# Four sums of weight blocks in each seven-product chunk: accumulating transfers on GpSimd's queue in place of VectorE additions

## The chip, the cores and the metric

The kernel runs on one core of one Trainium2 chip. A time is the device time of one execution, in microseconds (us); with one core there is no other to wait for. The core has TensorE (PE in the profile), VectorE (DVE), ScalarE (ACT), GpSimd (POOL) and a queue that only starts transfers (SP), each of which runs its own instructions in order and waits on semaphores for the others. Sixteen DMA engines move the data of all queues.

## What is computed

A two-layer encoder over 256 positions of width 2048, all in float32. Layer 0 mixes with grouped-query attention, layer 1 with dilated sliding-window attention in three head groups; each is followed by a gated MLP of width 5632 with a width-3 convolution over positions. Cut to what matters here:

```python
D_MODEL, SEQ, DEPTH, D_FF = 2048, 256, 2, 5632

def conv_ffn(h, w_up, conv_w, conv_b, w_down):
    u = h @ w_up                                   # 256x2048 @ 2048x11264
    u = depthwise_conv3(u, conv_w) + conv_b
    gate, val = jnp.split(u, 2, axis=-1)
    return (jax.nn.silu(gate) * val) @ w_down      # 256x5632 @ 5632x2048

def reference(x, ...):
    h = x
    for i in range(DEPTH):
        hn = rms_norm(h, mix_norm[i])
        h = h + (mixer_a(hn, ...) if i % 2 == 0 else mixer_b(hn, ...))
        h = h + conv_ffn(rms_norm(h, ffn_norm[i]), w_up[i], conv_w[i], conv_b[i], w_down[i])
    return rms_norm(h, final_norm)
```

Nearly all the work is the product of 256 rows of activations with some 420 MB of weights, each weight read once.

## The kernel before

**Loads and splits.** Weights arrive in `raw` tiles of 128 partitions x 2 x 512 float32 (512 KB), loaded by SP (`load_raw`, L137; `feed`, L146). There are six such buffers (`NRAW`), handed out in turn from a list (`new_raw`, `done_raw`). TensorE works here on operands of type fp32r, so each raw tile is split (`split_raw`, L126 to L133): ScalarE copies it to a high part `wh` (L129), VectorE subtracts that from the raw tile and leaves the low part `wl` (L130). A product is then three matmuls: high by high, high by low, low by high. There are three pairs of `wh`/`wl` buffers, four in the down projections, so a split runs at most that many pieces ahead of TensorE.

**Seven-product chunks.** A chunk is 512 rows of a weight matrix (`kg`) by two column blocks of 512 (`n0`, `n1`), seen as four blocks of one raw tile each: "11" and "12" are the first half of the rows in `n0` and `n1`, "21" and "22" the second half. Instead of eight block products, a chunk does seven, with sums of blocks (a Strassen scheme). The activations' sums (`forms`) are made earlier and are not touched. In `ORDER` the products are 1, 2, 5, 3, 7, 6, 4, and on the weights' side they take

- P1: 11; P2: 21; P3: 22, as they are stored
- P5: 11 + 12 (added into the tile of 11)
- P7: 12 + 22 (added into the tile of 12)
- P6: 22 + 11 + 12 (the sum of P5 added into the tile of 22)
- P4: 21 + 22 + 11 + 12 (the sum of P6 added into the tile of 21)

A tile that is added into must have been split before, since the split reads its old contents. A product of a chunk is six matmuls of 128x512. Between the products stand ordinary column blocks ("c" units, twelve matmuls). There are 23 chunks: seven in the MLP of layer 0, eight in that of layer 1, six in the query and key projections of layer 1, two in its output projection. All other chunks of weights go through `feed` or "c" units.

**What sets the order.** `project_pair` (L216) walks through a list of units. In each pass it loads the unit's block, calls `prepare` for the next unit, splits and multiplies. `prepare` (L246) issues the addition for the next unit if that is one of P5, P7, P6, P4 (table `sums`, L239; addition in L251), at high priority, so that a scheduler puts it ahead of other VectorE work. A scheduler then orders the instructions of each engine; within an engine they run in that order. TensorE's order is that of the units.

**GpSimd** has little to do: a part of the block placing after each 32x32 transpose (`place_blocks`, L361), 49 transfers of constants and biases of at most 256 KB, and some small operations.

Of the kernel before, what the change touches and what calls it, by code (L numbers as in the profile page):

```python
# [11 lines left out]
ALU = mybir.AluOpType  # L12
AX = mybir.AxisListType

P = 128
# [12 lines left out]
AHEAD = 45  # L28
# [6 lines left out]
def tile_encoder(ctx: ExitStack, tc: tile.TileContext, x, xT, w_a, w_ao, q_gain, k_gain, w_b, w_bo,  # L35
                 rel_bias, gains, w_up, conv, w_down, final_norm, rope, ident_c, onehot, out):
    nc = tc.nc
# [29 lines left out]
    def bank(i, name):  # L67
        return psp.tile([P, 512], F32, tag=f"b{i}", name=nm(name))

    def ps_tile():  # L70
        bank_at[1] = (bank_at[1] + 1) % 4
        return bank(4 + bank_at[1], "ps")
# [18 lines left out]
    def step():  # L91
        if wide:
            for g in pending[:2]:
                if next(g, StopIteration) is StopIteration:
                    pending.remove(g)
        while pending and not wide:
            if next(pending[0], StopIteration) is not StopIteration:
                return
            pending.pop(0)
        if spare and len(pending) < 2 and next(spare[0], StopIteration) is StopIteration:  # L100
            spare.pop(0)

    def drain(keep=0):
        while len(pending) > keep:
            step()
# [10 lines left out]
    def done_raw(t):  # L116
        free_raw.append(raw_tag.pop(id(t))[0])
# [3 lines left out]
    def new_hl():  # L121
        pool, i = hl_ring.pop(0)
        hl_ring.append((pool, i))
        return [pool.tile([P, 2, 512], F32R, tag=f"{t}{i}", name=nm(t)) for t in ("wh", "wl")]

    def split_raw(r, release=True):  # L126
        wh, wl = new_hl()
        with tc.high_priority(offset=AHEAD):
            nc.scalar.activation(wh, r, AF.Copy)  # L129
            nc.vector.tensor_tensor(wl, r, wh.bitcast(F32), ALU.subtract)  # L130
        if release:
            done_raw(r)
        return wh, wl  # L133

    def load_raw(w, n, kg, s):
        r = new_raw()
        nc.sync.dma_start(r.rearrange("p a c -> p (a c)"), w[n, kg][:, s * 1024:(s + 1) * 1024])  # L137
        return r
# [38 lines left out]
    def new_acc():  # L177
        bank_at[0] = (bank_at[0] + 2) % 4
        return [bank(bank_at[0] + m, "acc") for m in range(2)]
# [36 lines left out]
    def project_pair(w, n0, n1, lhs, forms, units, late, early_done, n0_done, product_done=None, tail=False,  # L216
                     lazy=False):
        home = {1: "M1", 2: "C11", 3: "C12", 4: "C21", 5: "M5", 6: "M6", 7: "M7"}
        if product_done or lazy:
            acc = dict(zip(("C11", "C21", "C12", "C22"), new_acc() + new_acc()))  # L220
        else:
            place = ("M1", "M5", "M6", "M7", "C11", "C21", "C12", "C22")
            if tail:
                place = ("C11", "C12", "C21", "C22", "M1", "M5", "M6", "M7")
            b = bank_at[0]
            acc = {k: bank((4, 5, 6, 7, 2 - b, 3 - b, b, b + 1)[i], "acc") for i, k in enumerate(place)}

        def touched(u):
            return (home[u[2]],) if u[0] == "P" else (("C11", "C21"), ("C12", "C22"))[u[2] // 2]

        first, last = {}, {}
        for i, u in enumerate(units):
            for k in touched(u):
                first.setdefault(k, i)
                last[k] = i
        if tail:
            last["C12"] = last["C22"] = None
        blocks = {}
        sums = {5: ("11", "12"), 7: ("12", "22"), 6: ("22", "11"), 4: ("21", "22")}  # L239

        def block(kg, b):
            if (kg, b) not in blocks:
                blocks[kg, b] = load_raw(w, (n0, n1)[int(b[1]) - 1], kg, int(b[0]) - 1)
            return blocks[kg, b]

        def prepare(u):  # L246
            kind, kg, p = u
            if kind == "P" and p in sums:
                dst, src = (block(kg, b) for b in sums[p])
                with tc.high_priority(offset=AHEAD):  # L250
                    nc.vector.tensor_tensor(dst, dst, src, ALU.add)  # L251
                if p == 6:
                    done_raw(blocks.pop((kg, "11")))
                elif p == 4:
                    done_raw(blocks.pop((kg, "22")))

        last_s = max(i for i, u in enumerate(units) if u[0] == "P")
        for i, (kind, kg, p) in enumerate(units):
            if i == late:
                drain()  # L260
            if kind == "c":
                r = load_raw(w, (n0, n1)[p // 2], kg, p % 2)
            else:
                b = {1: "11", 2: "21", 3: "22", 5: "11", 7: "12", 6: "22", 4: "21"}[p]
                r = block(kg, b)
            if i + 1 < len(units):
                prepare(units[i + 1])
            wh, wl = split_raw(r, kind == "c" or p in (7, 4))
            if kind == "P" and p in (7, 4):
                blocks.pop((kg, b))  # L270
            todo = []
            if kind == "c":
                for j in range(2):
                    for m, k in enumerate(touched((kind, kg, p))):
                        todo.append((k, *at(lhs[4 * kg + 2 * (p % 2) + j], m), j))
            else:
                f = forms(kg)[p]
                for j in range(2):
                    x = f[j] if isinstance(f, list) else [t[:, j * P:(j + 1) * P] for t in f]
                    todo.append((home[p], *x, j))  # L280
            for k, *_ in todo:
                if k not in acc:
                    acc[k] = bank(4 + ("M1", "M5", "M6", "M7").index(k), "acc") if lazy else ps_tile()
            fresh = {k for k in acc if first[k] == i}
            for k, xh, xl, j in todo:
                nc.tensor.matmul(acc[k], xh, wh[:, j, :], start=k in fresh, stop=False)  # L286
                fresh.discard(k)
                nc.tensor.matmul(acc[k], xl, wh[:, j, :], start=False, stop=False)  # L288
            todo.sort(key=lambda t: (t[0], t[3]))
            for k, xh, xl, j in todo:  # L290
                nc.tensor.matmul(acc[k], xh, wl[:, j, :], start=False, stop=last[k] == i and j == 1)  # L291
            if product_done and kind == "P" and home[p][0] == "M":
                product_done(home[p], acc.pop(home[p]))
            if i == last_s:
                early_done(acc)
            if i == max(last["C11"], last["C21"]):
                n0_done(acc)
            if not (product_done or lazy) or kind == "c" or p in (1, 5, 7, 4):
                step()
        return acc  # L300
# [14 lines left out]
    def at(e, m):  # L315
        return e[m] if isinstance(e, list) else tuple(t[:, m * P:(m + 1) * P] for t in e[:2])
# [56 lines left out]
    def seven(w, n0, n1, hT, forms, units, sums, n0_ready, n1_ready):  # L373
        (k0, k1), (q0, q1) = sums

        def product_done(k, t):
            if k != "M6":
                nc.scalar.activation({"M1": k0, "M5": q1, "M7": k1}[k], t, AF.Copy)
                return
            nc.vector.tensor_tensor(q0, t, k0, ALU.add)  # L380
            nc.vector.tensor_tensor(k1, k1, q0, ALU.add)
            nc.vector.tensor_tensor(q0, q0, q1, ALU.add)
            nc.vector.tensor_tensor(q1, k1, q1, ALU.add)

        def n0_done(a):
            nc.vector.tensor_tensor(k0, a["C11"], k0, ALU.add)
            nc.vector.tensor_tensor(k1, a["C21"], k1, ALU.add)
            n0_ready([k0, k1])

        a = project_pair(w, n0, n1, hT, forms, units, None, lambda a: None, n0_done, product_done)  # L390
        nc.vector.tensor_tensor(q0, a["C12"], q0, ALU.subtract)
        nc.vector.tensor_tensor(q1, a["C22"], q1, ALU.subtract)
        n1_ready([q0, q1])
# [431 lines left out]
    def out_proj(w, slots, kgs, late, g_next, junk, pool, tags, forms=None):  # L825
# [13 lines left out]
        def pair(n0, n1, units, late_at):  # L839
            def n0_done(a):  # L840
                finished(n0, n1)
                done((a["C11"], a["C21"]), n0)

            acc = project_pair(w, n0, n1, slots, lambda kg: forms, units, late_at,
                               lambda a: start(combine(a, n0, n1, pool, "stg", combined, 2)), n0_done, lazy=True)
            done((acc["C12"], acc["C22"]), n1)
# [533 lines left out]
```

## Time and profile before

| | us |
|---|---|
| median of 2 runs | 2235.53 (2235.5 and 2235.56) |
| the profiled execution, its span | 2235.3 |
| TensorE busy | 2222.8 |
| VectorE busy | 1838.0 |
| ScalarE busy | 1549.9 |
| GpSimd busy | 329.7 |

The result lists one time for each run and none for the profiled execution beyond its span; that lies 0.2 us under the median. The granted clock is 0.999 over the span. "Busy" is the union of an engine's instructions; "idle before" is the time in which it stood still just ahead of an instruction, and the name behind it is what ended that. A row of the timeline begins with its start and its length in us, and "x8" joins eight instructions alike.

### The profile page before, as it was taken

The page shows a single profiled execution, that of the slowest core. Times are in us where ns is not written, and L with a number is a line of the kernel's source. Part 1 is how long each engine was busy: PE and PEld are TensorE (multiplying, and loading weights), DVE is VectorE, ACT ScalarE, POOL GpSimd, SP SyncE. Part 2 cuts the span into 40 slices and gives each one's busy share as a digit, 9 for nine tenths or more (in the row PEclk, how much of TensorE's full clock was granted, in tenths as well). Part 3 has the DMA queues.
Part 4 walks back from the last instruction along what each step waited for, and adds up shares of the span by engine and source line. Part 5 has one row for each costly group of instructions (what it writes and reads, how often), then busy time and mean ns, then how long its engine had stood idle before and what let it go on. Part 6 is the DMA issues. An engine that isn't in the chain of part 4 may idle for free.

```text
span 2235.3 us, 29163 instructions
## 1 busy us (share of the span) xinstructions
PE 2222.8 (99%) x10021; PEld 1840.0 (82%) x10021; DVE 1838.0 (82%) x2523; ACT 1549.9 (69%) x2393; POOL 329.7 (15%) x482
## 2 busy tenths in 40 slices
PE   9999999999999999999999999999999999999998
PEld 7888888888888888888888888888888888888886
DVE  6777778888888788979877978786887898888897
ACT  7665677777557777767876777576777754677764
POOL 2210212210001010011340213010110100001101
PEclk9999999999999999999999999999999999999999
DMA  8444656766556665666655565565566666556654
GB/s 303 164 145 151 206 189 208 243 202 191 199 197 201 200 192 176 225 204 205 212 178 191 166 206 179 188 198 187 193 195 192 197 198 211 190 193 192 227 183 151
DMA packets 126501, 437.44 MB, mean 196 GB/s; under 512 B 17313, under 2 KB 18081, under 8 KB 126353
## 3 DMA queue, kind: packets, MB, share of 16 engines
q1 hardware_dynamic: 119744, 425.64, 58.1%
q0 software_dynamic: 6176, 9.39, 1.7%
q8 instruction: 78, 1.28, 0.2%
q14 instruction: 71, 0.57, 0.1%
q10 hardware_dynamic: 432, 0.56, 0.1%
HBM read 429.20 MB, written 6.29 MB: 195 GB/s over the span
## 4 chain that ended last, share of the span: by engine, by line
PE 93%; DVE 3%; issue 1%; DMA 1%; POOL 1%; ACT 1%; SPq 0%; DVEq 0%; POOLq 0%; ACTq 0%
PE acc L155 18%; PE acc L156 18%; PE acc L154 18%; PE acc L286 11%; PE acc L291 11%; PE acc L288 11%; DVE wl L130 2%; DMA raw<-in_w_down_dram 1%; PE ps L291 1%; PE ps L321 1%; PE ps L286 1%; PE ps L288 1%; PE ps L325 0%; POOL pp L361 0%; PE ps L324 0%
## 5 line engine op out<-in xcount | busy, mean ns | idle before, releaser
L130 DVE TENSOR_TENSOR wl<-raw,wh 128x1024 fp32r<-128x1024 f32 x861 | 1056.8, 1234 | 266.4 <-ACT wh L129 262.3
L129 ACT ACTIVATE wh<-raw 128x1024 fp32r<-128x1024 f32 x861 | 902.6, 1057 | 467.5 <-PE acc L156 166.3
L154 PE MATMUL acc<-wh,xh 128*128 128x512 f32 x1664 | 649.2, 391 | 0.0
L155 PE MATMUL acc<-wl,xh 128*128 128x512 f32 x1664 | 648.8, 390 | 0.3 <-DVE wl L130 0.2
L156 PE MATMUL acc<-wh,xh 128*128 128x512 f32 x1664 | 648.1, 389 | 0.0
L155 PEld LDWEIGHTS acc<-wl,xh 128*128 128x128 f32 x1664 | 312.6, 188 | 67.4 <-DVE wl L130 2.8
L156 PEld LDWEIGHTS acc<-wh,xh 128*128 128x128 f32 x1664 | 312.4, 188 | 64.6
L154 PEld LDWEIGHTS acc<-wh,xh 128*128 128x128 f32 x1664 | 312.7, 188 | 63.7 <-ACT wh L165 0.3
L286 PE MATMUL acc<-wh,ah 128*128 128x512 f32 x762 | 297.0, 390 | 0.6 <-DVE h L544 0.6
L288 PE MATMUL acc<-wh,al 128*128 128x512 f32 x762 | 296.7, 389 | 0.0
L361 POOL COPY u<-t 32x256 f32<-32x256 f32 x176 | 110.5, 628 | 1003.9 <-DVE t L591 995.7
L291 PE MATMUL acc<-wl,ah 128*128 128x512 f32 x762 | 212.0, 389 | 0.4 <-DVE wl L130 0.4
L286 PEld LDWEIGHTS acc<-wh,ah 128*128 128x128 f32 x762 | 143.1, 188 | 31.2 <-DVE h L544 1.5
L291 PEld LDWEIGHTS acc<-wl,ah 128*128 128x128 f32 x762 | 143.0, 188 | 30.4 <-DVE wl L130 0.9
L288 PEld LDWEIGHTS acc<-wh,al 128*128 128x128 f32 x762 | 143.1, 188 | 29.5
L286 PE MATMUL acc<-wh,xh 128*128 128x512 f32 x416 | 162.7, 391 | 0.0
L288 PE MATMUL acc<-wh,xh 128*128 128x512 f32 x416 | 162.0, 389 | 0.0
L363 ACT ACTIVATE u<-t 32x256 f32<-32x256 f32 x352 | 147.6, 419 | 17.8 <-DVE t L591 9.9
L251 DVE TENSOR_TENSOR raw<-raw,raw 128x1024 f32<-128x1024 f32 x92 | 112.8, 1226 | 14.8 <-DMA raw<-in_w_down_dram 14.1
L291 PE MATMUL acc<-wl,xh 128*128 128x512 f32 x416 | 113.1, 390 | 0.0
L288 PEld LDWEIGHTS acc<-wh,xh 128*128 128x128 f32 x416 | 78.1, 188 | 16.0
L286 PEld LDWEIGHTS acc<-wh,xh 128*128 128x128 f32 x416 | 78.1, 188 | 16.0
(254 smaller groups left out, 2388.9 us busy)
## 6 DMA issues: line engine op xcount, KB each, us to landing
raw<-in_w_up_dram SPq DMA_DIRECT2D x352, 512.0 KB, 4.5
raw<-in_w_down_dram SPq DMA_DIRECT2D x176, 512.0 KB, 4.9
raw<-in_w_b_dram SPq DMA_DIRECT2D x144, 512.0 KB, 4.5
raw<-in_w_bo_dram SPq DMA_DIRECT2D x48, 512.0 KB, 4.4
raw<-in_w_a_dram SPq DMA_DIRECT2D x40, 512.0 KB, 4.5
raw<-in_w_ao_dram SPq DMA_DIRECT2D x32, 512.0 KB, 3.8
raw<-in_w_a_dram SPq DMA_DIRECT2D x16, 256.0 KB, 6.1
h<-in_x_dram SPq DMA_DIRECT2D x4, 512.0 KB, 8.4
```

The costliest lines, as they stand in the source:

```text
L129: nc.scalar.activation(wh, r, AF.Copy)
L130: nc.vector.tensor_tensor(wl, r, wh.bitcast(F32), ALU.subtract)
L154: nc.tensor.matmul(accs[m], xh, wh[:, j, :], start=st, stop=False)
L155: nc.tensor.matmul(accs[m], xh, wl[:, j, :], start=False, stop=False)
L156: nc.tensor.matmul(accs[m], xl, wh[:, j, :], start=False, stop=sp)
L251: nc.vector.tensor_tensor(dst, dst, src, ALU.add)
L286: nc.tensor.matmul(acc[k], xh, wh[:, j, :], start=k in fresh, stop=False)
L288: nc.tensor.matmul(acc[k], xl, wh[:, j, :], start=False, stop=False)
L291: nc.tensor.matmul(acc[k], xh, wl[:, j, :], start=False, stop=last[k] == i and j == 1)
L321: nc.tensor.matmul(o, lh[ls], rh[rs], start=start, stop=stop)
L361: nc.gpsimd.tensor_copy(dst, src)
L363: nc.scalar.activation(dst, src, AF.Copy)
```

## The change

`prepare` goes. In its place `sum_next` runs behind the split of a product and issues the next sum as a transfer with `accum_op=ALU.add` on GpSimd's queue: the sixteen DMA engines read the source and the destination, and write back the sum. P5's and P7's second operand is read from memory (`stored`), so blocks 12 and 22 are read twice, once to be added and once into a tile of their own; P6's and P4's is read from a tile (`flat`). Blocks 12 and 22 are also loaded earlier in the list, behind P1 and P5, and the tile of 11 is given back behind P3, that of 22 behind P6.

```diff
-        sums = {5: ("11", "12"), 7: ("12", "22"), 6: ("22", "11"), 4: ("21", "22")}
...
-        def prepare(u):
-            kind, kg, p = u
-            if kind == "P" and p in sums:
-                dst, src = (block(kg, b) for b in sums[p])
-                with tc.high_priority(offset=AHEAD):
-                    nc.vector.tensor_tensor(dst, dst, src, ALU.add)
-                if p == 6:
-                    done_raw(blocks.pop((kg, "11")))
-                elif p == 4:
-                    done_raw(blocks.pop((kg, "22")))
+        def add_onto(kg, b, src):
+            dst = blocks[kg, b].rearrange("p a c -> p (a c)")
+            nc.gpsimd.dma_start(dst, src, accum_op=ALU.add)
+
+        def stored(kg, b):
+            s = int(b[0]) - 1
+            return w[(n0, n1)[int(b[1]) - 1], kg][:, s * 1024:(s + 1) * 1024]
+
+        def flat(kg, b):
+            return blocks[kg, b].rearrange("p a c -> p (a c)")
+
+        def sum_next(kg, p):
+            if p == 1:
+                add_onto(kg, "11", stored(kg, "12"))
+                block(kg, "12")
+            elif p == 5:
+                add_onto(kg, "12", stored(kg, "22"))
+                block(kg, "22")
+            elif p == 3:
+                add_onto(kg, "22", flat(kg, "11"))
+                done_raw(blocks.pop((kg, "11")))
+            elif p == 7:
+                add_onto(kg, "21", flat(kg, "22"))
+            elif p == 6:
+                done_raw(blocks.pop((kg, "22")))
...
-            if i + 1 < len(units):
-                prepare(units[i + 1])
             wh, wl = split_raw(r, kind == "c" or p in (7, 4))
+            if kind == "P":
+                sum_next(kg, p)
```

Below, the four sums of a chunk are called sum 5, 7, 6 and 4 after the product that takes them. Lines of the changed kernel are 14 higher from here on; the transfers are issued in its L247.

First place: the second chunk (first down projection of layer 0), VectorE, before. Its tiles are 5320 (block 11), 5346 (12), 5393 (22) and 5332 (21); 5405, 5434 and 5463 are column blocks.

```order
L130 TENSOR_TENSOR wl_5396<-raw_5393,wh_5395 128x1024 [waits PE_49,Activation_49]
L307 TENSOR_TENSOR fm_5554<-xs_5551,fm_5554 128x256 [waits Activation_49]
L251 TENSOR_TENSOR raw_5393<-raw_5393,raw_5320 128x1024 [waits DVE_49]
L130 TENSOR_TENSOR wl_5409<-raw_5405,wh_5408 128x1024 [waits DMAHW3_49,PE_49,Activation_49]
L130 TENSOR_TENSOR wl_5425<-raw_5346,wh_5424 128x1024 [waits PE_49,Activation_49]
L251 TENSOR_TENSOR raw_5332<-raw_5332,raw_5393 128x1024 [waits DVE_49]
L130 TENSOR_TENSOR wl_5438<-raw_5434,wh_5437 128x1024 [waits DMAHW4_49,PE_49,Activation_49]
L130 TENSOR_TENSOR wl_5454<-raw_5393,wh_5453 128x1024 [waits PE_49,Activation_49]
L130 TENSOR_TENSOR wl_5467<-raw_5463,wh_5466 128x1024 [waits DMAHW6_49,PE_49,Activation_49]
L130 TENSOR_TENSOR wl_5483<-raw_5332,wh_5482 128x1024 [waits PE_49,Activation_49]
```

The same place in the changed kernel, GpSimd's queue and then VectorE's; the tiles are now 5320 (11), 5327 (12), 5370 (22) and 5335 (21). A semaphore with SW in its name is one of GpSimd's transfers, with HW one of SP's; the first row is still sum 4 of the chunk ahead.

```order
L247 DMA raw_5134<-raw_5180 128x1024 [waits DMAHW2_49,DMASW2_49,DMASW1_49]
L247 DMA raw_5327<-in_w_down_dram 128x1024 [waits DMAHW2_49,DMAHW3_49,DMAHW0_49,DMAHW6_49,DMASW3_49,DVE_49]
L247 DMA raw_5320<-in_w_down_dram 128x1024 [waits DMASW7_49,DMAHW5_49,DMASW4_49,DVE_49]
L247 DMA raw_5370<-raw_5320 128x1024 [waits DMASW5_49,DMASW4_49,DMAHW1_49,DMASW2_49,DVE_49]
L247 DMA raw_5335<-raw_5370 128x1024 [waits DMAHW7_49,DMASW6_49,DMASW5_49]
```

```order
L130 TENSOR_TENSOR wl_5397<-raw_5370,wh_5396 128x1024 [waits DMAHW1_49,PE_49,Activation_49]
L130 TENSOR_TENSOR wl_5410<-raw_5407,wh_5409 128x1024 [waits DMAHW3_49,PE_49,Activation_49]
L130 TENSOR_TENSOR wl_5426<-raw_5327,wh_5425 128x1024 [waits DMASW3_49,PE_49,Activation_49]
L130 TENSOR_TENSOR wl_5439<-raw_5436,wh_5438 128x1024 [waits DMAHW4_49,PE_49,Activation_49]
L130 TENSOR_TENSOR wl_5455<-raw_5370,wh_5454 128x1024 [waits DMASW5_49,PE_49,Activation_49]
L130 TENSOR_TENSOR wl_5467<-raw_5464,wh_5466 128x1024 [waits DMAHW6_49,PE_49,Activation_49]
L130 TENSOR_TENSOR wl_5483<-raw_5335,wh_5482 128x1024 [waits DMASW6_49,PE_49,Activation_49]
```

The additions have left VectorE. On GpSimd's queue sum 7 stands first, then sums 5, 6 and 4, and the last waits for the landing of sum 6 (DMASW5); the splits of P7, P6 and P4 now wait for transfers.

Second place: the third chunk of layer 1's query and key projections, GpSimd before. `kT` and `qT` are copies of `place_blocks` for the head group ahead.

```order
L361 COPY kT_9686<-tT_9687 32x8x32 [waits DVE_49,PE_49]
L361 COPY kT_9686<-tT_9687 32x8x32 x7
L361 COPY qT_9792<-tT_9793 32x8x32 [waits DVE_49]
L361 COPY qT_9792<-tT_9793 32x8x32 x7
L1140 DMA btg_8909<-scr_98 128x4x128 [waits DMASW3_49,DVE_49]
```

GpSimd in the changed kernel at that place; the chunk's tiles are 9822 (11), 9829 (12), 9900 (22) and 9865 (21).

```order
L247 DMA raw_9829<-in_w_b_dram 128x1024 [waits DMAHW3_49,DMAHW5_49,DMASW5_49,DVE_49]
L375 COPY kT_9686<-tT_9687 32x8x32 [waits DVE_49,PE_49]
L375 COPY kT_9686<-tT_9687 32x8x32 x7
L375 COPY qT_9792<-tT_9793 32x8x32 [waits DVE_49]
L375 COPY qT_9792<-tT_9793 32x8x32 x6
L247 DMA raw_9822<-in_w_b_dram 128x1024 [waits DMAHW2_49,DMAHW1_49,DMAHW6_49,DMAHW0_49,DVE_49]
L375 COPY qT_9792<-tT_9793 32x8x32
L247 DMA raw_9900<-raw_9822 128x1024 [waits DMAHW1_49,DMASW6_49,DMAHW7_49,DMASW0_49,DVE_49]
L247 DMA raw_9865<-raw_9900 128x1024 [waits DMAHW5_49,DMASW7_49]
```

Sum 5 (into 9822) stands behind seven of the eight copies to `qT`, where before VectorE added it with no copy of GpSimd ahead of it. Of the 23 chunks four have GpSimd copies like these just ahead of sum 5.

Third place: SP's queue between the first and the second chunk, before.

```order
L137 DMA raw_5273<-in_w_down_dram 128x1024 [waits DMAHW1_49,DVE_49]
L137 DMA raw_5302<-in_w_down_dram 128x1024 [waits DMAHW6_49,DMAHW4_49,DVE_49]
L137 DMA raw_5320<-in_w_down_dram 128x1024 [waits DMAHW5_49,DVE_49]
L137 DMA raw_5332<-in_w_down_dram 128x1024 [waits DMAHW2_49,DVE_49]
L137 DMA raw_5344<-in_w_down_dram 128x1024 [waits DMAHW0_49,DVE_49]
```

SP's queue there in the changed kernel; 5274 is the column block between P6 and P4 of the first chunk.

```order
L137 DMA raw_5302<-in_w_down_dram 128x1024 [waits DMAHW1_49,DVE_49]
L137 DMA raw_5274<-in_w_down_dram 128x1024 [waits DMAHW4_49,DMASW1_49,DMASW0_49]
L137 DMA raw_5320<-in_w_down_dram 128x1024 [waits DMAHW5_49,DMASW7_49,DVE_49]
L137 DMA raw_5327<-in_w_down_dram 128x1024 [waits DMAHW2_49,DVE_49]
L137 DMA raw_5335<-in_w_down_dram 128x1024 [waits DMAHW7_49,DMASW2_49,DVE_49]
```

Three loads of the next blocks now wait for sums of this chunk (6, 7 and 4 in that order), since their buffers held the sums' tiles; what stands behind them on SP waits with them.

## The prediction

> **What bounds the kernel now.** I read the busy times first, then TensorE's waits, then the timeline at the chunks. In the busy times the reader is to see that TensorE leaves 12.5 us of the 2235.3 us span, and what the splits and the additions take:
>
> ```profile
> PE 2222.8 (99%) x10021; PEld 1840.0 (82%) x10021; DVE 1838.0 (82%) x2523; ACT 1549.9 (69%) x2393; POOL 329.7 (15%) x482
> q1 hardware_dynamic: 119744, 425.64, 58.1%
> L130 DVE TENSOR_TENSOR wl<-raw,wh 128x1024 fp32r<-128x1024 f32 x861 | 1056.8, 1234 | 266.4 <-ACT wh L129 262.3
> L129 ACT ACTIVATE wh<-raw 128x1024 fp32r<-128x1024 f32 x861 | 902.6, 1057 | 467.5 <-PE acc L156 166.3
> L251 DVE TENSOR_TENSOR raw<-raw,raw 128x1024 f32<-128x1024 f32 x92 | 112.8, 1226 | 14.8 <-DMA raw<-in_w_down_dram 14.1
> ```
>
> All of TensorE's named waits, its line first, then what it waited for, the total, the count and the longest:
>
> ```profile
> PE ps L511 <- DVE warm L508: 1.5, 1, 1.5
> PE ps L325 <- DVE qTl L307: 0.6, 1, 0.6
> PE acc L286 <- DVE h L544: 0.6, 1, 0.6
> PE acc L291 <- DVE wl L130: 0.4, 1, 0.4
> PE acc L155 <- DVE wl L130: 0.4, 2, 0.2
> ```
>
> TensorE is the bound. It waited 0.8 us in all for splits (the rows of `wl`), so VectorE, 82% busy, costs nothing that relief could give back. A gain is bounded by the 12.5 us and more likely by the 0.8; the median of the runs (2235.53) lies 0.2 us over this span, so the sum is made against 2235.5. About 2% (45 us) is what a measurement of this kernel can tell from no change.
>
> **What goes.** 92 additions of 1.226 us, 112.8 us of VectorE. They stand beside TensorE's work, so their going is worth nothing; the 0.8 us I leave out. All sums move to GpSimd's queue and the DMA engines, where I look for what is late next.
>
> **What each sum has for a deadline.** A product can start when its sum has landed and ScalarE has copied it, and its low part must be there four matmuls later. By the rows of L129 and L130 that is 1.06 + 1.23 us, less four matmuls that start 0.23 us apart (568.18 and 568.41 below): a sum must land 1.38 us before its product. It may start when the old contents of its tile are split. For the first chunk (four rows) and the second (seven rows), in order of time and VectorE's ahead of TensorE's: end of P1's split, end of P3's split, then the starts of P5 and P4, in the second chunk with P6 between them.
>
> ```profile
> 530.68 1.23 DVE L130 TENSOR_TENSOR wl<-raw,wh 128x1024 fp32r<-128x1024 f32 x1
> 541.94 1.22 DVE L130 TENSOR_TENSOR wl<-raw,wh 128x1024 fp32r<-128x1024 f32 x1
> 542.34 0.39 PE L286 MATMUL acc<-wh,ah 128*128 128x512 f32 x1
> 558.66 0.39 PE L286 MATMUL acc<-wh,ah 128*128 128x512 f32 x1
> ...
> 558.18 1.22 DVE L130 TENSOR_TENSOR wl<-raw,wh 128x1024 fp32r<-128x1024 f32 x1
> 569.04 1.22 DVE L130 TENSOR_TENSOR wl<-raw,wh 128x1024 fp32r<-128x1024 f32 x1
> 568.18 0.39 PE L286 MATMUL acc<-wh,ah 128*128 128x512 f32 x1
> 568.41 0.39 PE L288 MATMUL acc<-wh,al 128*128 128x512 f32 x1
> 580.42 0.39 PE L286 MATMUL acc<-wh,ah 128*128 128x512 f32 x1
> 584.50 0.39 PE L286 MATMUL acc<-wh,ah 128*128 128x512 f32 x1
> ```
>
> Second chunk: sum 5 has 568.18 - 1.38 - 559.40 = 7.4 us. Sums 6 and 4 follow one another, sum 4 waiting on GpSimd's queue for the landing of sum 6; sum 6 alone has 580.42 - 1.38 - 570.26 = 8.8 us, the pair 584.50 - 1.38 - 570.26 = 12.9 us. First chunk: 9.1 and 14.1 us. Sum 7 waits for no split, only for a load that lands well before; I cost it at nothing, its cover being the two products ahead of P7.
>
> At four chunks GpSimd's own copies stand ahead of sum 5. The third of layer 1's projections, with GpSimd's copies, the old addition, and P5's start:
>
> ```profile
> 1070.03 7.22 POOL L361 COPY qT<-tT 32x256 f32<-32x256 f32 x8 [1.44 <-DVE tT L351]
> 1071.53 1.30 DVE L251 TENSOR_TENSOR raw<-raw,raw 128x1024 f32<-128x1024 f32 x1
> 1080.49 0.39 PE L286 MATMUL ps<-wh,sf 128*128 128x512 f32 x1
> ```
>
> Seven of eight copies end at 1076.35, so sum 5 starts 4.8 us later than the addition did and has 1080.49 - 1.38 - 1076.35 = 2.8 us.
>
> The last chunk's pair, from the end of P3's split (2195.39) to P4's start, has 12.0 us:
>
> ```profile
> 2193.04 2.35 DVE L130 TENSOR_TENSOR wl<-raw,wh 128x1024 fp32r<-128x1024 f32 x2
> 2208.81 0.39 PE L286 MATMUL acc<-wh,ah 128*128 128x512 f32 x1
> ```
>
> Read off the timeline in the same way for all 23 chunks, in order, us: sum 5 has 9.1, 7.4, 9.9, 11.5, 10.5, 9.1, 6.1, 10.8, 5.1, 2.8, 11.1, 6.0, 2.8, 12.7, 9.9, 9.1, 7.4, 9.9, 11.5, 10.5, 9.1, 6.0, 8.2; the pair has 14.1, 12.9, 12.9, 13.9, 10.8, 9.9, 9.6, 10.1, 13.8, 14.4, 15.3, 14.9, 14.4, 13.3, 11.1, 14.1, 12.4, 12.9, 13.5, 10.8, 9.9, 8.4, 12.0 (mean 12.4).
>
> **What a sum takes.** No accumulating transfer is in this trace. The nearest rows, with the median from issue to landing at the end:
>
> ```profile
> raw<-in_w_down_dram SPq DMA_DIRECT2D x176, 512.0 KB, 4.9
> fin<-in_final_norm_dram POOLq DMA_DIRECT2D x4, 256.0 KB, 5.1
> bt<-scr POOLq DMA_DIRECT2D x8, 256.0 KB, 6.4
> btg<-scr POOLq DMA_DIRECT2D x4, 256.0 KB, 6.7
> ```
>
> The price of bytes follows from the row of queue q1: 58.1% of 2235.3 us for 425.64 MB is 1.6 us of all sixteen engines for 512 KB. The nearest in queue and shape is `fin` (GpSimd's queue, 128 rows from memory): 5.1 us for half the bytes. The other half adds 0.8, and the destination, which must be read back, 512 KB more, 1.6: 7.5 us. Lower end: the read-back costs nothing, 5.9. Upper end: reading back and adding take as long as a whole load again, 2 x 4.9 = 9.8. I take 7.5, since the rows show time that grows with bytes on these engines, and keep both ends. [...]
>
> **The sum.** At 7.5 us, sum 5 is short at eight chunks by 16.5 us in all, 9.5 of it at the two with 2.8 us. The pair needs 15.0 us and is short at 22 of 23, by 59.9 us in all, 2.6 on average. What TensorE stands still there is lost, since it has no other slack: 2235.5 + 16.5 + 59.9 = 2312 us. With 5.9 us a sum it is 7 + 14 = 21 us (2256), with 9.8 us 39 + 165 = 205 us (2440).
>
> Costed at nothing: GpSimd's time to issue 92 transfers, contained in the landing times; the second reading of blocks 12 and 22, 46 x 512 KB, as far as the engines have room (see the second rival); the loads on SP that wait for sums. The column block behind P6 is such a load: it starts when sum 6 lands and takes 4.9 us, so it needs 12.4 us from P3's split where the pair needs 15.0, and is due 2.7 us before P4 in most chunks. The two run out together, and TensorE stands still once for both. Behind ScalarE's wait for a sum stand the copies of the next blocks on its queue, and VectorE's subtractions behind those; they have the lead that the split buffers gave, which such a wait uses up. I add nothing for it.
>
> **Rivals.** *The transfer is as short as a plain one.* The point at which it decides is 6.8 us a sum, where the shortfalls sum to 45 us. For it speaks that reads and writes of one transfer may overlap, and the SP row's 4.9 us for 512 KB. Against it, GpSimd's rows take 5.1 to 6.7 us for half of that. With 5.9 us: 2256, not slower than a measurement can tell. [...]
>
> *The DMA engines fill up.* The row of the first four chunks, with its length, the engines' busy times, the clock, the DMA share and GB/s:
>
> ```profile
> 537.00:650.00 113.00, 112.42 (x496) 92.75 (x495) 100.94 (x114) 59.79 (x65) 0.00 (x0) 1.00 0.61 205
> ```
>
> They are busy for 0.61 x 113 = 69 us. Sixteen sums at 1.6 us for the source and 1.6 for the read-back add 51: 120 us in 113. Then loads and sums delay one another, a sum takes 9.8 us or more, and column blocks come late too: 2440 or more. [...]
>
> *TensorE gains from a free VectorE.* It would have to be waiting for it; with 0.8 us of such waits, and 12.5 us at the very most (2223), this cannot pass 2%.
>
> **How the numbers follow.** A sum of 6.8 to 9 us, the forecast: 0.45. The short transfer, up to 6.8: 0.28. The full engines, over 9: 0.26. A gain over 2%: 0.01. So slower 0.71, same 0.28, faster 0.01. The likeliest case gives 2312, its own range 2280 to 2393 (at 9 us the shortfalls are 29 + 129). The range for 8 in 10 reaches from 2245, under the short transfer's 2256, to 2440, the upper end.
>
> **What would show it.** Right: the rows of the accumulating transfers read 7 to 8 us from issue to landing; TensorE waits at L300 and L305 for splits, 2 to 3 us at most chunks, mostly at P4 and the column block behind P6, and about 5 us at the two chunks with copies ahead of sum 5; `wh` (L129) waits for `raw` transfers of GpSimd; VectorE's busy time is 113 us less and TensorE's stays at 2223. The first rival shows as landings under 6.8 us and hardly any waits; the second as loads by SP that land in much more than 4.9 us, and waits of TensorE at column blocks far from any sum. The prediction is wrong if the sums land on time and TensorE stands still elsewhere, or if they take more than 10 us.

## The result, and the profile after

The changed kernel takes 2434.44 us (median of 2433.09 and 2435.78), the one before 2235.53: a ratio of 1.0888, 95% interval 1.0856 to 1.092. It is slower by 199 us. The forecast was slower by 76 us; 2434 lies inside the range that was given, near its upper end.

The page of the changed kernel, with the rows that answer to those shown of before (the lines of the code stand 14 further down, so L300, L302 and L305 are the three matmuls of a product that were L286, L288 and L291):

```profile
PE 2290.0 (94%) x10021; PEld 1861.3 (76%) x10021; DVE 1735.4 (71%) x2431; ACT 1541.8 (63%) x2393; POOL 400.9 (16%) x574
q1 hardware_dynamic: 119744, 425.64, 53.5%
q0 software_dynamic: 19424, 57.63, 12.7%
L302 PE MATMUL acc<-wh,al 128*128 128x512 f32 x762 | 308.3, 405 | 0.0
raw<-in_w_down_dram SPq DMA_DIRECT2D x176, 512.0 KB, 5.2
raw<-raw POOLq DMA_DIRECT2D x46, 512.0 KB, 8.5
raw<-in_w_down_dram POOLq DMA_DIRECT2D x26, 512.0 KB, 8.5
```

VectorE lost 103 us of work (113 were forecast), and that bought nothing. TensorE stands still for 2434.0 - 2290.0 = 144.0 us of the span where it was 12.5 before (131.5 more), and it is busy for 67.2 us longer with the same 10021 matmuls. These two are the 199 us. The second was not foreseen: matmuls that take longer than 0.39 us show in the mean of 405 ns of L302, where the same group of before had 389:

```profile
L288 PE MATMUL acc<-wh,al 128*128 128x512 f32 x762 | 296.7, 389 | 0.0
```

The waits of the changed kernel, in us in total, count and longest; TensorE's, ScalarE's and SP's queue:

```profile
PE acc L300 <- ACT wh L129: 112.1, 46, 8.5
PE ps L300 <- ACT wh L129: 9.5, 5, 3.1
PE acc L155 <- DVE wl L130: 2.9, 7, 1.5
...
ACT wh L129 <- DMA raw<-raw: 166.4, 37, 10.3
...
SPq L137 <- DMA raw<-raw: 278.5, 43, 10.3
```

TensorE waits for ScalarE's copies, and ScalarE for `raw<-raw`, the sums 6 and 4, whose source is a tile. The last row is the one to keep in mind: SP, too, stood for 278.5 us before loads that needed the tile of a running sum.

The timeline at the second chunk: GpSimd's issue of sums 6 and 4, SP's loads in the same moment, then P4 on TensorE.

```profile
581.32 0.86 POOL L247 DMA_DIRECT2D raw<-raw  x1 [13.96 <-DVE wl L130]
588.95 0.86 POOL L247 DMA_DIRECT2D raw<-raw  x1 [6.77 <-DMA raw<-raw]
...
588.72 1.28 SPq L137 DMA_DIRECT2D raw<-in_w_down_dram  x3
...
600.20 0.80 PE L300 MATMUL acc<-wh,ah 128*128 128x512 f32 x1 [3.17 <-ACT wh L129]
600.79 0.63 PE L302 MATMUL acc<-wh,al 128*128 128x512 f32 x1
601.22 0.63 PE L300 MATMUL acc<-wh,ah 128*128 128x512 f32 x1
601.65 0.63 PE L302 MATMUL acc<-wh,al 128*128 128x512 f32 x1
602.07 1.06 PE L305 MATMUL acc<-wl,ah 128*128 128x512 f32 x2
602.93 0.47 PE L300 MATMUL acc<-wh,ah 128*128 128x512 f32 x1
```

When sum 6 lands (588.7), SP issues three loads within 0.9 us, and GpSimd issues sum 4. What the sixteen engines then move, in the first 5.1 us and in the 4.5 us after that (queue: packets, MB, share):

```profile
q1 hardware_dynamic: 235, 0.90, 73.9%
q14 instruction: 1, 0.01, 0.6%
...
q0 software_dynamic: 140, 0.52, 59.0%
q1 hardware_dynamic: 190, 0.68, 41.5%
```

For 5.1 us not one packet of sum 4 moves, only SP's loads (0.90 of their 1.5 MB); then the two share the engines. Sum 4 lands at 599.0, and P4 starts 1.2 us later. Its matmuls start 0.43 us apart (600.79, 601.22, 601.65) until 602.9 and 0.23 us apart from then on. In the whole trace 225 starts are 0.35 to 0.52 us apart where 25 were before, which makes some 40 of the 67 us of longer busy time; what the rest is made of was not tried.

From issue to landing, and from issue to the first packet, taken transfer by transfer from the records of the DMA engines, medians over the 23 chunks, us (sum 5 mostly starts while packets of sum 7 still move on the same queue, so its own first packet can't be told):

| | sum 7 | sum 5 | sum 6 | sum 4 | sum 6's issue to sum 4's landing |
|---|---|---|---|---|---|
| lands after | 8.2 | 7.5 | 6.5 | 10.2 | 16.7 |
| first packet after | 2.7 | | 1.4 | 5.1 | |
| the shortest landing | 5.4 | 5.5 | 4.7 | 8.7 | |

### The profile page after: what moved, and what is told of

It reads as the page before. It is cut to its first block, busy times and chain, and to the rows that moved or that the text cites. A ratio compares the mean times of both kernels' runs of the same rounds, so it can differ in the third digit from the quotient of the medians.

```text
span 2434.0 us, 29303 instructions
## 1 busy us (share of the span) xinstructions
PE 2290.0 (94%) x10021; PEld 1861.3 (76%) x10021; DVE 1735.4 (71%) x2431; ACT 1541.8 (63%) x2393; POOL 400.9 (16%) x574
## 3 DMA queue, kind: packets, MB, share of 16 engines
q0 software_dynamic: 19424, 57.63, 12.7%
## 5 line engine op out<-in xcount | busy, mean ns | idle before, releaser
L300 PE MATMUL acc<-wh,ah 128*128 128x512 f32 x762 | 313.8, 412 | 80.7 <-ACT wh L129 76.3
L302 PE MATMUL acc<-wh,al 128*128 128x512 f32 x762 | 308.3, 405 | 0.0
L300 PEld LDWEIGHTS acc<-wh,ah 128*128 128x128 f32 x762 | 150.5, 197 | 128.0 <-ACT wh L129 91.4
L305 PE MATMUL acc<-wl,ah 128*128 128x512 f32 x762 | 221.9, 404 | 0.9
L300 PE MATMUL acc<-wh,xh 128*128 128x512 f32 x416 | 171.5, 412 | 35.8 <-ACT wh L129 35.8
L305 PEld LDWEIGHTS acc<-wl,ah 128*128 128x128 f32 x762 | 147.2, 195 | 38.9 <-DVE wl L130 8.3
L302 PEld LDWEIGHTS acc<-wh,al 128*128 128x128 f32 x762 | 150.4, 197 | 31.1
L302 PE MATMUL acc<-wh,xh 128*128 128x512 f32 x416 | 167.5, 403 | 0.0
L300 PEld LDWEIGHTS acc<-wh,xh 128*128 128x128 f32 x416 | 82.0, 197 | 60.9 <-ACT wh L129 44.0
L305 PE MATMUL acc<-wl,xh 128*128 128x512 f32 x416 | 116.2, 397 | 1.1 <-DVE wl L130 0.8
L247 POOL DMA_DIRECT2D raw<-raw x46 | 39.7, 864 | 399.3 <-DVE wl L130 270.2
L302 PEld LDWEIGHTS acc<-wh,xh 128*128 128x128 f32 x416 | 81.9, 197 | 16.8
```

The source lines that it names most:

```text
L247: nc.gpsimd.dma_start(dst, src, accum_op=ALU.add)
```

## Experiments

Theory: sum 4 is late because SP, whose queue runs in order, stood still for sum 6 and lets its loads go in the moment in which sum 4 is issued; and TensorE's clock falls when it waits, which adds the rest. Rivals: the second readings of blocks 12 and 22 fill the engines; a second sum in a row, tile onto tile, is slow by its own nature; the slow matmuls come from the transfers' traffic, not from the clock.

In the first kernels, and in one further on, a sum is a transfer if it stands in the tuple `VIA`, and is VectorE's addition of before if not:

```diff
+VIA = (7, 5)
...
             if p == 1:
-                add_onto(kg, "11", stored(kg, "12"))
+                if 5 in VIA:
+                    add_onto(kg, "11", stored(kg, "12"))
...
+            if kind == "P" and p in SUMS and p not in VIA:
+                dst, src = (block(kg, b) for b in SUMS[p])
+                with tc.high_priority(offset=AHEAD):
+                    nc.vector.tensor_tensor(dst, dst, src, ALU.add)
```

**Sums 7 and 5 as transfers** (`VIA = (7, 5)`)

> Sums 7 and 5 stay transfers, sums 6 and 4 go back to VectorE. Theory: of the 199 us, the serial pair of sums 6 and 4 costs most: the waits at P4, P6 and column blocks (115 us) and the clock that falls behind them. They go; what is left is the 17 us at P5 and some 8 us of slow clock behind it: 2260 us (2248 to 2275), and the P5 waits are the same seven. Rival, the DMA engines fill up because blocks 12 and 22 are read twice: the second readings are all still there, so waits at column blocks stay and the time is 2300 us or more.

Measured: 2279.11 us, ratio 1.0184 [1.0167, 1.0201], 42 us over before, 19 more than the theory's middle and 4 over its range. P4 and the column blocks wait for nothing; TensorE's waits are those at P5. So 42 of the 199 us belong to sums 7 and 5 (to sum 5, by the run of sum 7 alone further on), and the pair adds 157 to them.

**Sums 6 and 4 as transfers** (`VIA = (6, 4)`)

> The other half: sums 6 and 4 as transfers, 7 and 5 on VectorE, so that no block is read twice. Theory of the pair: waits at P4 and column blocks stay as they are, only the 17 us at P5 and the slow clock behind them go: 2410 us (2390 to 2425). Rival, the second readings fill the engines: with 46 x 512 KB less to read the pair lands in about 13 us and the time falls to 2330 us or less.

Measured: 2306.67 us, 1.0309 [1.0294, 1.0324], which looks like the rival's number and is not. VectorE's sum 7 came behind sum 6 here, so P7 took a block 22 with a sum already in it and waited for that (35 us in all, at 20 chunks), and sum 4, issued behind P7's split, came when only one load went out with it, 0.3 us ahead: its first packet after 2.3 us, its landing after 6.7. The second kernel has sum 7 ahead, with `EARLY = {3: 7}`:

```diff
+            if kind == "P" and p in EARLY:
+                prepare(("P", kg, EARLY[p]))
...
```

> Sums 6 and 4 as transfers, 7 and 5 on VectorE, this time with VectorE's sum 7 ahead of sum 6 (in the run sums64 it came behind sum 6 and took in the wrong contents of block 22, and P7 waited for it). No block is read twice. Theory, the serial pair: sum 4 starts right behind the landing of sum 6, together with SP's loads, and the pair takes 16 us or more; only what sums 7 and 5 cost by themselves goes (43 us by the run sums75): 2392 us (2370 to 2410). Rival, the second readings fill the engines: the pair lands in 13 us and the time is 2330 us or less.

Measured: 2373.9 us, 1.0612 [1.0596, 1.0628], inside the theory's range. Sum 4's first packet still comes 4.9 us after its issue, it lands after 10.2 us, and the pair takes 16.1. With no block read twice the pair is as slow as ever: the second readings are not the cause. 137 us here and 42 us above make 179 of the 199.

**Sum 6 alone back on VectorE** (`VIA = (7, 5, 4)`)

> Only sum 6 goes back to VectorE; sums 7, 5 and 4 are transfers. In the changed kernel sum 4 moves its first packet 5.1 us after its issue, and 1.5 MB of loads by SP pass in between. Theory: these are loads that SP held back behind its own wait for the landing of sum 6, released in the same moment. With sum 6 on VectorE, SP is not held, sum 4's first packet comes 1.5 to 3 us after its issue and it lands in 7 to 8 us instead of 10.2; P4 has about 11 us for it, so its waits go and the time is 2265 us (2250 to 2285). Rival, sum 4 is slow by its own nature (second in a row, both of its operands in tiles): the first packet still takes 5 us, the landing 10 us, P4 still waits here and there: 2290 us or more.

Measured: 2298.44 us, 1.0275 [1.026, 1.029]. The addition came behind sum 4 here, so that P4 went without what sum 6 adds, and sum 4 waited for no other sum: it landed after 6.8 us. With the addition ahead of it, `EARLY = {7: 6}`:

> Only sum 6 on VectorE, added in the pass of P7 ahead of sum 4 (in the run sum6_vector it came behind, and sum 4 took in a block 22 that was not yet summed). Sums 7, 5 and 4 are transfers. Theory, sum 4 was slow because of the loads released at the same moment: its first packet comes 1 to 2 us after its issue, it lands in 7 us, and the time is that of sums 7 and 5 alone, 2280 us (2270 to 2300). Rival, sum 4 starts late by its own nature: 5 us to the first packet, 10 us to the landing, 2310 us or more.

Measured: 2325.0 us, 1.0398 [1.038, 1.0415]. The first packet comes after 2.0 us, as the theory said, the landing after 8.3 us, between the two. The time lies in the rival's range (2310 or more). SP's loads still go out around sum 4, since VectorE's addition releases both, but they are spread: 0.5 us ahead of its issue and 0.6 and 1.7 us behind it, where in the changed kernel it was 0.2 ahead and 0.2 and 0.7 behind. 1.5 MB of them pass before sum 4 has landed. So the start is not late by nature, but this run alone does not decide what the landing costs.

**Sum 4 alone back on VectorE** (`VIA = (7, 5, 6)`)

> Only sum 4 on VectorE; sums 7, 5 and 6 are transfers. Theory: sum 6 lands in 5.5 to 6.5 us, inside the 8.8 us that P6 leaves it, and VectorE's sum 4 is done 1.2 us later, so P4 no longer waits. But SP still stands before the load that takes the tile of 11 until sum 6 has landed, and the column block behind P6 is held there: 20 to 35 us of waits stay at column blocks: 2305 us (2290 to 2325). Rival, SP's holding costs nothing: the time of sums 7 and 5 alone, 2280 us or less.

Measured: 2322.22 us, 1.0383 [1.0368, 1.0399], inside the theory's range, 43 us over sums 7 and 5 alone. Its waits are only in part where they were expected: some 15 us at column blocks (20 to 35 were expected), while those at P5 grew from 25 to 31.

**Tile of 11 given back later**

```diff
             elif p == 3:
                 add_onto(kg, "22", flat(kg, "11"))
-                done_raw(blocks.pop((kg, "11")))
             elif p == 7:
                 add_onto(kg, "21", flat(kg, "22"))
+                done_raw(blocks.pop((kg, "11")))
```

> All four sums as transfers, but the tile of 11 goes back on the list of free buffers behind P7 and no longer behind P3. SP's loads then take other tiles first, and the one that must wait for sum 6 comes later in SP's order. Theory, SP's holding is part of the cost: fewer loads are released at the moment in which sum 4 is issued, its first packet comes sooner than 5.1 us, and the time falls by 10 to 60 us, to 2375 to 2425 us. Rival, the holding costs nothing or only moves to the release of the tile of 22 at sum 4's landing: 2434 us or more.

Measured: 2427.53 us, 1.0856 [1.0839, 1.0872], 7 us less than the changed kernel, which the intervals do not separate; it lies between the theory's range and the rival's. The three loads still go out at sum 6's landing, and sum 4's first packet comes after 4.9 us. But the place of the waits changed: TensorE's at column blocks fell from 36 to 5 us, and those at P4 rose from 73 to 103 us, the same in all.

**The loads held back until sum 4 is issued.** As above, and a small instruction on GpSimd keeps the tile of 11 for a moment longer:

```diff
+    touch = cpool.tile([P, 8], F32, name="touch")
...
                 add_onto(kg, "21", flat(kg, "22"))
+                nc.gpsimd.tensor_tensor(touch, blocks[kg, "22"][:, 0, :8], blocks[kg, "11"][:, 0, :8], ALU.add)
                 done_raw(blocks.pop((kg, "11")))
```

> As late_release, and GpSimd reads eight columns of the tiles of 11 and 22 right behind its issue of sum 4, so that the tile of 11 is free for SP only then, some 1 to 1.5 us after the landing of sum 6. Theory, sum 4 is late because three loads by SP, released at the landing of sum 6, reach the engines ahead of it: held back, they come behind it; its first packet comes 1 to 2 us after its issue (4.9 in late_release), it lands in 7 to 8.5 us (10.0), the waits at P4 fall by about 2 us a chunk, and the time falls from 2428 to 2365 to 2400 us. First rival, sum 4 starts late by its own nature: 5 us and 10 us as before, 2425 us or more. Second rival, the loads now come late by as much: the landing is short, but the column blocks wait instead, 2420 us or more.

Measured: 2344.41 us, 1.0483 [1.0469, 1.0498]: 83 us less than the kernel above, from one instruction more in each chunk. Sum 4's first packet comes after 1.4 us (4.9), it lands after 4.8 us (10.0), and the pair takes 11.7 us (16.6). The second chunk again, GpSimd's and SP's rows of the timeline, and behind them what the engines moved from 587.3 to 590.7, while sum 4 ran:

```profile
585.90 0.86 POOL L248 DMA_DIRECT2D raw<-raw  x1 [5.41 <-DMA raw<-raw]
586.46 1.62 POOL L268 TENSOR_TENSOR touch<-raw,raw 128x8 f32<-128x8 f32 x1
...
588.10 1.32 SPq L138 DMA_DIRECT2D raw<-in_w_down_dram  x2
```

```profile
q0 software_dynamic: 144, 0.52, 85.4%
q1 hardware_dynamic: 50, 0.17, 18.8%
```

The loads now go out at 588.1, 2.2 us after sum 4, and come behind it on the engines. Both rivals fall. The gain is larger than the forecast 28 to 63 us: sum 4 lands after 4.8 us where 7 to 8.5 were forecast. The loads which stand behind sum 4's own landing are released sooner too, which is likely a part of it: SP's waits for `raw<-raw` at L138 are 101.4 us where those at L137 were 270.6 in the kernel above.

**Copies in place of sums**

```diff
-            nc.gpsimd.dma_start(dst, src, accum_op=ALU.add)
+            nc.gpsimd.dma_start(dst, src)
```

> The changed kernel with all 92 transfers as plain copies, which overwrite the tile and add nothing; all else is the same, so the sums of the blocks are left out. The prediction gave the read-back of the destination 1.6 us of each sum. By the trace a sum holds the sixteen engines for 2.9 us and a load for 1.6, a difference of 1.3. Theory: each transfer lands 1 to 1.6 us sooner, the pair 2 to 3 us, and the time falls by 45 to 75 us to 2360 to 2390 us. Rival, reading back lies beside the writing and costs next to nothing: landings within 0.5 us and 2420 us or more.

Measured: 2305.8 us, 1.0315 [1.03, 1.033], 129 us less than the changed kernel, far more than the forecast. GpSimd's queue held the engines for 7.6% of 2301.6 us where it was 12.7% of 2434.0, which is 134 us less, 1.46 us for each of the 92. The landings came 1.6 to 2.7 us sooner, the pair 5 us (11.7). Copies that no load disturbed landed in 2.9 us, sums in 4.7. SP's loads go out at the landing of sum 6's copy as before, and the first packet of sum 4's copy comes after 3.5 us (5.1).

**One sum that nobody waits for** (`VIA = (7,)`)

> Only sum 7 is a transfer, the other three are VectorE's additions. It reads 23 x 512 KB a second time and waits for nothing but loads. Theory: a sum that nobody waits for costs nothing, as the prediction had it: within 4 us of the kernel before. Rival, its 23 x 2.9 us of the sixteen engines delay loads that are needed: 10 us or more slower.

Measured: 2236.08 us, 0.9999 [0.999, 1.0008]. Theory right. It reads 23 blocks a second time and takes 24 us from VectorE, and neither shows.

**TensorE kept busy while it waits.** Two kernels fill the waits with matmuls of zeros, to show whether the clock then stays up. In the changed kernel, 42 places:

```diff
+            k, xh, _, _ = todo[0]
+            for _ in range(FILL.get(count[0], 0)):
+                nc.tensor.matmul(acc[k], xh, zeros, start=k in fresh, stop=k in fresh)
+            count[0] += 3 * len(todo)
             for k, xh, xl, j in todo:
                 nc.tensor.matmul(acc[k], xh, wh[:, j, :], start=k in fresh, stop=False)
```

> The changed kernel with 474 more matmuls (zeros as the moving operand, added onto sums or ahead of their start, so that no result changes), put into the 42 places where TensorE stood still for over 1 us in the profile, each place filled to within 0.3 us of its wait. Theory: the matmuls that start 0.43 us apart instead of 0.23 behind such waits (some 45 to 55 us in all) are TensorE's clock, which falls when it stands still; with the places filled it does not fall, the mean of the matmuls at L302 goes from 0.40 to 0.39 us, the granted clock from 0.977 to 0.99 or more, and the time falls by 20 to 50 us, though 108 us of work is added; it falls by less than the 50 where the data then come late by as much. Rival, the slow starts come from the transfers (their traffic in the tiles that the matmuls read): the 0.43 us stay, and the time is the same or longer.

Measured: 2429.45 us, 1.0858 [1.0842, 1.0874], 5 us less than the changed kernel. The page's row of TensorE, the groups of the zeros, and the timeline at the place that was P4 of the second chunk:

```profile
PE 2365.8 (97%) x10483; PEld 1926.2 (79%) x10483; DVE 1737.5 (72%) x2432; ACT 1543.1 (64%) x2393; POOL 398.4 (16%) x574
```

```profile
L306 PE MATMUL acc<-zero,ah 128*128 128x512 f32 x295 | 71.3, 389 | 0.0
L306 PE MATMUL acc<-zero,xh 128*128 128x512 f32 x131 | 31.2, 389 | 0.0
L306 PE MATMUL ps<-zero,sf 128*128 128x512 f32 x27 | 6.6, 389 | 0.0
L306 PE MATMUL ps<-zero,fm 128*128 128x512 f32 x9 | 2.3, 395 | 0.0
```

```profile
598.42 3.11 PE L306 MATMUL acc<-zero,ah 128*128 128x512 f32 x13
601.37 0.39 PE L309 MATMUL acc<-wh,ah 128*128 128x512 f32 x1
601.60 0.39 PE L311 MATMUL acc<-wh,al 128*128 128x512 f32 x1
```

Behind the zeros P4 starts its matmuls 0.23 us apart. The granted clock rose from 0.977 to 0.993, so most of the slow starts were the clock, and the transfers' traffic (the rival) did not make them. Without the 111.4 us of zeros TensorE is busy for 2254.4 us, 35.6 less. But what it waits, zeros included, is 62.4 + 111.4 = 173.8 us where it was 144.0: 29.8 us came back as waiting. The forecast of 20 to 50 us was wrong; only 5.8 us of span are left.

The same in the kernel of sums 7 and 5:

> The kernel of sums75 (2279 us) with 89 matmuls of zeros in the seven places where TensorE stood still for over 0.9 us, each filled to within 0.3 us of its wait. Some 16 us of its 42 us over the kernel before are slow starts behind these waits. Theory, the fallen clock is lost where no later sum or load makes TensorE wait anyway: with one late sum a chunk it shows, and the time falls by 8 to 16 us to 2263 to 2271 us. Rival, as in the run fill what the clock gives is waited away at the next sum: 2275 us or more.

Measured: 2274.62 us, 1.0171 [1.0158, 1.0185], 4.5 us less than without the zeros; the intervals overlap. The granted clock is 0.999 and the slow stretches are gone. The time lies 0.4 us under the rival's bound and 3.6 over the theory's range: of the 12.2 us that TensorE got back here (2240.8 us busy without zeros, 2249.9 - 21.3 = 2228.6 with them), 6.7 were waited away and 5.5 are left.

## Why the prediction was right and wrong

*TensorE is the bound, and relief for VectorE is worth nothing:* right. One sum taken from VectorE changes the time by 0.01%, four leave it 103 us less to do.

*Sum 7 is free:* right, by the same run.

*Sum 5 is short at eight chunks, 16.5 us:* mostly right in place, small in size. In the changed kernel TensorE waited 17.3 us at P5, at seven chunks, six of them among the eight; that the totals agree is luck. GpSimd's copies held the issue back by 3.3 to 3.7 us at three of the seven (where the waits were 1.8 to 3.2 us, not 5), and P5 started 1.2 us after the landing where it had to wait. But in the kernel of sums 7 and 5 the time rose by 42: waits of 25 us (the landings' mean was 8.1 us, not 7.5), and 18 us by which TensorE was busy longer.

*The pair is short by 59.9 us:* wrong, 137 us by itself and 157 on top of sums 7 and 5. Where TensorE fell behind, by the starts of its matmuls against those of before, us over the 23 chunks:

| stretch | changed | 11 given back later | loads held back | sums 7 and 5 alone |
|---|---|---|---|---|
| P2 to P5 | 20 | 20 | 44 | 25 |
| P5 to P3 | 11 | 10 | 18 | 15 |
| P6 to P4, with the column block | 114 | 106 | 16 | 0 |
| P4 to the next chunk's P1 | 38 | 44 | 16 | 0 |
| the rest | 16 | 14 | 13 | 3 |
| all | 199 | 195 | 108 | 43 |

The step that failed stands among those "costed at nothing": "the loads on SP that wait for sums". The prediction saw that such a load stands behind sum 6 and asked only when that load comes. It did not ask what goes out when SP is let go: three loads at once, 1.5 MB, into the engines that sum 4 needs. With the loads held back until sum 4 was under way the third row falls from 106 to 16 us, and the time by 83 us. The pair took 16.7 us where the sum had 15.0. Put chunk by chunk into the prediction's own sum, the measured pairs are short by 98 us. The rest is lateness for which the sum had no term, above all the 38 us behind P4. The loads that get ahead are not enough by themselves: the plain copies have the same loads let go, and with 1.46 us less of the engines for each transfer they are 129 us faster. So both count: a sum that holds the engines for long, and the loads ahead of it. That "TensorE stands still once for both" was right: given back later, the tile of 11 moved some 30 us of waits from the column block to P4, and the time hardly changed.

*A sum takes 7.5 us:* the step that hid this. The price was put together from rows of other transfers, as if it were the transfer's own. A sum that little else disturbed landed in 4.7 us, a copy in 2.9, below the lower end of 5.9. Over the 92 sums of the changed kernel, the landing is about 4.6 us and 0.96 times the engine time that SP's loads took in between (correlation 0.94; part of it is built in, since a longer landing has room for more loads). So 7.5 us came out for sum 5 (median 7.5), too much for sum 6 (6.5) and too little for sum 4 (10.2, over the 10 us at which the prediction called itself wrong), by what else was on the engines. No run shows the read-back of 1.6 us by itself; what they show is that a sum holds the engines for 1.46 us longer than a copy, whatever that is made of.

*"TensorE's stays at 2223":* wrong, it is 2290, and 35.6 of the 67 us are the clock by the run that fills the waits. It falls behind the longer waits: slow starts in 23 stretches of 2.1 to 5.6 us at the chunks, where the trace of before has none but at its start. The granted clock reads 0.5 there (0.50 from 600 to 602 us, at P4 of the second chunk), for 3.41 or 6.83 us each time, and the starts go from 0.23 to 0.43 us. In this trace the clock changes on a grid of 3.41 us, and the ends of the stretches lie on it within 0.7 us. TensorE was busy for 0 to 1.73 us of the 3.41 ahead of each of the 23 falls, with one wait of 1.6 us or one of 0.9 and one of 1.0 in the shortest cases, while waits of 3.0 and 3.2 us that lay across two steps of the grid passed without a fall. The slow time is not all a loss on top of the waiting: in the fill run, of 35.6 us that the clock gave back, 29.8 were waited for the next sum; in the kernel of sums 7 and 5 it was 6.7 of 12.2.

*The leads behind ScalarE's wait, "I add nothing for it":* part of the same miss. P1's split ended 3.3 us before P1 on average and 2.4 us in the changed kernel, P3's 2.1 and 1.4 us, and the windows of the next sums shrink by so much.

*The rivals.* The short transfer is half right and does not help: with the loads held back the pair takes 11.7 us, as with 5.9 us a sum, which was to give 2256; the time is 2344, for lateness then shows at P5 (44 us). Why sum 5's landings reach 11.8 us in that kernel was not tried. The undisturbed copies took 2.9 us for 512 KB, and the rows of 5.1 to 6.7 us for 256 KB that the prediction held against a short transfer had loads in them, which held 0.41 to 0.75 of the engines. Full engines, the second rival, are there only for moments: in the second chunk the DMA share is 0.95 from 590.5 to 598, once SP is let go, and 0.02 from 587.7 to 589.5, just before that. The loads themselves land nearly as before (5.2 us and 4.9), so that mechanism was not the one. The upper end of 2440, near which the time came out, was made with 9.8 us for each sum, where the medians are 6.5 to 10.2; that it held the time is luck.

## What to carry to other kernels

A transfer that others wait for had no price of its own here (sum 4 landed after 10.0 us, and after 4.8 with the loads held back): ask what else is released by the event that releases it, and in which order the engines get the two. SP's queue, which waited for one transfer, sent what it held (three loads, 1.5 MB, within 0.9 us) in the same moment in which the next was issued; holding that back by a microsecond or two was worth 83 us here. And time that a slower engine seems to lose behind a wait is only lost as far as no later wait would have taken it anyway (29.8 of 35.6 us came back as waiting).

## What the runs showed of the hardware that was not expected

While a sum ran with few loads beside it, the engines were full at 171 GB/s, about half the rate of loads (383). In these rows of windows, DMA share and GB/s are the last two columns. First sum 6 of the changed kernel, which moved 0.51 of the 0.65 MB in the window:

```profile
582.70:586.50 3.80, 3.80 (x18) 3.15 (x17) 1.82 (x2) 1.06 (x1) 0.00 (x0) 1.00 1.02 171
```

Then a stretch of loads in the kernel that holds them back:

```profile
591.00:596.00 5.00, 5.00 (x24) 4.14 (x23) 4.12 (x5) 3.93 (x4) 0.00 (x0) 1.00 1.01 383
```

171 GB/s against 383 is 0.45. Over the whole run a sum held the sixteen engines for 2.9 us (12.7% of 2434.0 us, less the queue's 1.7% of 2235.3 before, by 92), and a copy by the same queue for 1.5 (7.6% of 2301.6, less the same): again about half the rate.

Loads issued by SP 0.2 us before, 0.2 and 0.7 us behind sum 4 kept its first packet back for 5 us; issued 2.2 us behind it they did not. So here loads passed a GpSimd transfer that was issued before them: 0.90 MB of SP's moved in the 5.1 us in which none of sum 4 did, and the one load issued ahead of sum 4 has 0.52. A part of that is the start: where the engines were empty, a load's first packet came 1.0 us after its issue, and that of an undisturbed sum 1.4. What else sets the order within the engines no run here shows.
